# A pair's seventh operand formed earlier, its low parts on VectorE, and its last product behind the next pair's first, in the second layer's seven-product stages

## The chip, the cores and the metric

The kernel runs on one core of one Trainium2 chip. The time is that of one execution on the device, in microseconds (us). Three runs of the kernel before gave 2354.08, 2358.27 and 2360.64; the median, 2358.27, is its time.

## The reference, cut to what matters

Two layers (DEPTH = 2) of a mixer and a SwiGLU run over 512 latent tokens and 256 context tokens. The second layer needs only the latent tokens. The stages that the change touches are the branch gates' projection `g` and the two first projections of the SwiGLU, all of them products of the layer's activations with a large weight matrix:

```
def merge_branches(ys, g, w_branch, w_out):
    proj = jnp.einsum('bngi,gio->bngo', y, w_branch)
    gate = jax.nn.sigmoid(g.reshape(b, n, N_BRANCH, D_MODEL)...)
    return jnp.sum(gate * proj, axis=2) @ w_out

def swiglu(h, w_gate, w_up, w_down):
    return (jax.nn.silu(h @ w_gate) * (h @ w_up)) @ w_down
```

Here D_MODEL is 1024 and the SwiGLU's hidden width 2816, which is 22 blocks of 128 columns.

## The kernel before, in words

Every fp32 factor is split into a high part, rounded to TensorE's fp32r format, and a low part, the difference. A product of two factors is three matmuls: high by high, low by high, high by low. ScalarE casts a weight tile of 128x512 to its high part (`whi`, L220); a subtraction on VectorE or GpSimd makes the low part (`wlo`, L221).

For two neighbouring blocks of 128 output columns (a pair), the kernel doesn't multiply eight quarter matrices but seven, after Strassen and Winograd. The function `seven` (L478) lays out these products. The pair's weights are two tiles of 128x1024, `r0` and `r1`, of which each holds two quarters: a11 and a12, a21 and a22. `quarter` (L224) forms the weight operand of product q = 0 to 6: a11; a11 - a21 (written over a21); the sum s2 = a21 + a22 - a11; a12; the sum s1 = a21 + a22; a22; and a12 - s2, written over a12. L230 is the first sum s1, which needs both tiles; L231, L234 and L236 are the subtractions. The activations' sums (`tp`) are formed once for a stage by `sums` (L432 on). A product is 12 matmuls (four slices of 128 rows, three matmuls each), 84 for a pair. In layer 1 such a matmul has 384 columns (half of 768 tokens), in layer 2 256.

The products gather in three PSUM banks: the first, third, fifth and last in one (`y`), the second and sixth in another, the fourth in a third. ScalarE copies what a bank holds after the first three products (`p`, L491), and VectorE adds these copies back: L497 after the fourth product, L500 after the fifth, L502 after the sixth. So the last product's matmuls may not write bank `y` before the add at L500 has read it. In the FFN, gate pairs then go through the SiLU on ScalarE; the results of up pairs are multiplied by it, two of them on GpSimd (L1984) and one on VectorE (L1976).

`LO_POOL` tells which of a pair's seven low parts GpSimd forms: the first, fourth and sixth in layer 1, the fourth alone in layer 2. All others are VectorE's.

Weights come from HBM by loads of 512 KB on SyncE's queue (L213). They go round a ring of tiles, `raw` and `xraw`: four in layer 1, five in layer 2. A load waits until the tile that it overwrites has been read for the last time. `split_to` (L240) orders the loads and operands: a step asks for its own operand and the next four.

The stages are lists of steps, and a scheduler then sets each engine's order by a timeline of its own; within an engine, instructions run in that order. Some groups of steps are pinned against each other; the pairs' products are not.

In the FFN (L1892 on) the pairs run for f = 2, 4, ..., 20, each time gate then up: 20 pairs. After f = 12, layer 2 reloads two hidden tiles (`reload`). Ahead of the pairs lie two columns in the plain manner (L287, L296); behind them comes the down projection (L2056). The gate pairs of layer 2's mixer (L1606 on) are five.

Of the kernel before, what the change touches and what calls it, by code (L numbers as in the profile page):

```python
# [29 lines left out]
NF = FH // P  # L30
# [16 lines left out]
MID = ((), (3,))  # L47
PB = 1
PB = 1
LO_POOL = ((0, 3, 5), (3,))  # L50
MOD_NA = (4, 5)
MOD_FFN = ((8, 9), (10, 11))
THP = 2
# [90 lines left out]
class Kern:  # L144
# [37 lines left out]
    def drive(self):  # L182
        nc = self.nc
# [33 lines left out]
        def split(x, n, hi_eng, lo_eng, l=None):  # L217
            hi = ring(l, [P, 512], "whi", F32R, WB, XW)
            lo = ring(l, [P, 512], "wlo", F32R, WB, XW)
            hi_eng(hi[:, :n], x)  # L220
            lo_eng.tensor_sub(lo[:, :n], x, hi[:, :n].bitcast(F32))  # L221
            return hi, lo

        def quarter(pair, q):  # L224

            r0, r1 = raw[pair.r0], raw[pair.r0 + 1]
            a11, a12, a21, a22 = r0[:, :512], r0[:, 512:], r1[:, :512], r1[:, 512:]
            if q == 1:
                pair.sums[1] = self.t("fx", [P, 512], "ss", F32, 3)
                nc.vector.tensor_add(pair.sums[1], a21, a22)  # L230
                nc.vector.tensor_sub(a21, a11, a21)  # L231
            elif q == 2:
                pair.sums[2] = self.t("fx", [P, 512], "ss", F32, 3)
                nc.vector.tensor_sub(pair.sums[2], pair.sums[1], a11)  # L234
            elif q == 6:
                nc.vector.tensor_sub(a12, a12, pair.sums[2])  # L236
            x = (a11, a21, pair.sums.get(2), a12, pair.sums.get(1), a22, a12)[q]
            return Block([split(x, 512, nc.scalar.copy, nc.gpsimd if q in LO_POOL[pair.l] else nc.vector, pair.l)], 512)

        def split_to(n):  # L240
            while state[1] < min(n, len(reqs)):
                i = state[1]
                src, k, kind, r, pool, lo = reqs[i]
                if kind == "pair":
                    load_to(src.r0 + RAWB + XRAW[src.l])
                    got[i] = quarter(src, k)
                    if k == 6:
                        load_to(src.r0 + 1 + RAWB + XRAW[src.l])
                else:
                    load_to(r + 1)  # L250
                    x = raw.pop(r)
                    size = 416 if k == 832 else min(k, 512)
                    got[i] = Block([split(x[:, c:c + size], size, nc.gpsimd.tensor_copy if pool else nc.scalar.copy,
                                          nc.vector if lo else nc.gpsimd) for c in range(0, k, size)], size)
                    load_to(r + RAWB)
                state[1] += 1
# [221 lines left out]
    def seven(self, l, src, tp, dest, direct, added):  # L478
# [28 lines left out]
        def product(q, n, k, c):  # L507
# [16 lines left out]
        n_to_t = {6: 2, 7: 3, 4: 4}  # L524
        return [product(q, n, k, c) for q, (n, k, c) in enumerate(
            ((1, 0, e), (7, 0, None), (6, 0, None), (2, 4, e), (5, 0, d), (4, 0, None), (3, 4, d)))]


    def mod_steps(self, l, nb):
# [1362 lines left out]
    def ffn(self, l):  # L1892
# [70 lines left out]
        def pair_steps(up, f0):  # L1963
# [17 lines left out]
            def added(i, cols):  # L1981
                t = dest(i)[:, cols]
                if up:
                    nc.gpsimd.tensor_mul(t, t, s["sg", f0 + i][:, cols])  # L1984
                    if i == 1:
                        h_done(f0 + i)
                else:
                    nc.scalar.activation(t, t, AF.Silu)
# [23 lines left out]
                hs[f] = self.t("fd" if cx else "hk", [P, tt], f"h{f}")  # L2012
                nc.sync.dma_start(hs[f], self.hbuf[f][:, :tt])

        main = []
        for f in range(2, NF, 2):
            main += pair_steps(False, f) + pair_steps(True, f)
            if f == NA - 2 and not cx:
                main += [Step(reload)]
        st += main  # L2020
        st += [self.close("ft", "fx"), self.open("fd", "right")]

        if cx:
# [220 lines left out]
```

## Time and profile before

| what | value |
|---|---|
| median of three runs | 2358.27 us |
| the profiled execution's time | 2349.7 us |
| its span, first to last instruction | 2347.9 us |
| TensorE matmuls busy | 2258.5 us, 96% |
| VectorE busy | 1288.7 us, 55% |
| ScalarE busy | 1097.6 us, 47% |
| GpSimd busy | 922.7 us, 39% |
| mean granted TensorE clock | 0.989 |
| layer 2's gate pairs | 1783 to 1838 us of the span |
| layer 2's FFN pairs | 1985 to 2210 us of the span |

PE is TensorE, DVE VectorE, ACT ScalarE, POOL GpSimd, SP SyncE, which here only issues loads. In a group of instructions, `out<-in` are the program's names; after the bar come busy time, mean ns of one, and the idle time of the engine just before them with what ended it. A name such as `raw<-in_w_up_dram` is a load. Line numbers are those of the kernel before; in the order of the changed kernel they are 1 to 9 higher.

### The profile page before, as it was taken

The numbers are of one execution on the slowest core, as the hardware profiler recorded it, in microseconds if no ns is written. First come the engines' busy times: TensorE is split into PE (matmuls) and PEld (weight loads), VectorE is DVE, ScalarE is ACT, GpSimd is POOL, SyncE is SP. The second block draws the span as 40 slices with busy tenths as digits, with TensorE's granted clock in tenths as the row PEclk, the third lists the DMA queues.
The fourth block names the chain that finished last, engine by engine and source line by source line (L and its number), as shares of the span: only waits on it lengthen the run. The fifth ranks groups of instructions, "written<-read, shape, count | busy, mean of one in ns | idle before, by whom it ended". The sixth has DMA issues, their size and how long they took to land. (4 is left out here: it accounts for less than half of the span.)

```text
span 2347.9 us, 36358 instructions
## 1 busy us (share of the span) xinstructions
PE 2258.5 (96%) x13806; PEld 1960.9 (84%) x13806; DVE 1288.7 (55%) x2403; ACT 1097.6 (47%) x2434; POOL 922.7 (39%) x685
## 2 busy tenths in 40 slices
PE   7999999999999999999999999999999999999997
PEld 5877788878998889999987888787778878999875
DVE  7345456655424487556532272445578257888544
ACT  5346567634422254444442253675675325545532
POOL 1231153112258434334448362325301773323483
PEclk9999999999999999999999999999999999999998
DMA  9366321117676432222162342223224843323342
GB/s 356 117 228 217 126 95 62 68 63 268 210 275 227 142 135 84 99 99 86 63 246 72 108 155 83 76 89 100 79 73 176 299 153 139 117 93 103 111 153 63
DMA packets 113466, 323.43 MB, mean 138 GB/s; under 512 B 12966, under 2 KB 24172, under 8 KB 113292
## 3 DMA queue, kind: packets, MB, share of 16 engines
q1 hardware_dynamic: 89900, 269.34, 33.1%
q10 hardware_dynamic: 20160, 46.49, 5.2%
q0 software_dynamic: 3232, 5.28, 0.8%
q8 instruction: 108, 1.77, 0.3%
q14 instruction: 66, 0.54, 0.1%
HBM read 269.92 MB, written 55.35 MB: 139 GB/s over the span
## 5 line engine op out<-in xcount | busy, mean ns | idle before, releaser
L221 POOL TENSOR_TENSOR wlo<-raw,whi 128x512 fp32r<-128x512 f32 (+2 forms) x413 | 572.3, 1393 | 895.3 <-ACT whi L220 833.0
L220 ACT CAST whi<-raw 128x512 fp32r<-128x512 f32 (+1 forms) x449 | 274.0, 616 | 441.4 <-PE ps L1702 86.4
L519 PE MATMUL ps<-tp,whi 128*128 128x384 f32 (+1 forms) x1088 | 267.6, 315 | 0.2 <-ACT whi L220 0.2
L519 PE MATMUL ps<-AH,whi 128*128 128x384 f32 (+1 forms) x628 | 197.1, 316 | 7.2 <-DVE hx L500 4.1
L287 PE MATMUL ps<-AH,whi 128*128 128x512 f32 (+1 forms) x616 | 195.0, 362 | 3.3 <-ACT AH L738 3.3
L519 PE MATMUL ps<-AH,wlo 128*128 128x384 f32 (+1 forms) x628 | 196.4, 313 | 0.0
L519 PE MATMUL ps<-AL,whi 128*128 128x384 f32 (+1 forms) x628 | 194.8, 312 | 0.0
L519 PEld LDWEIGHTS ps<-tp,whi 128*128 128x128 f32 x1088 | 191.0, 189 | 2.1 <-PE ps L519 0.4
L287 PE MATMUL ps<-AH,wlo 128*128 128x512 f32 (+1 forms) x616 | 190.7, 357 | 0.0
L287 PE MATMUL ps<-AL,whi 128*128 128x512 f32 (+1 forms) x616 | 190.1, 356 | 0.0
L519 PE MATMUL ps<-tp,wlo 128*128 128x384 f32 (+1 forms) x544 | 171.0, 314 | 0.6 <-DVE wlo L221 0.6
L2056 PE MATMUL ps<-whi,hx 128*128 128x512 f32 x520 | 161.9, 390 | 7.3 <-DVE hx L2049 3.3
L335 PE MATMUL ps<-wlo,AH 128*128 128x512 f32 (+1 forms) x352 | 135.2, 384 | 0.8 <-POOL wlo L221 0.8
L335 PE MATMUL ps<-whi,AL 128*128 128x512 f32 (+1 forms) x352 | 135.7, 385 | 0.0
L335 PE MATMUL ps<-whi,AH 128*128 128x512 f32 (+1 forms) x352 | 134.0, 388 | 1.6 <-ACT whi L220 1.6
L519 PEld LDWEIGHTS ps<-AH,whi 128*128 128x128 f32 x628 | 119.0, 190 | 11.6 <-DVE hx L500 5.0
L287 PEld LDWEIGHTS ps<-AH,whi 128*128 128x128 f32 x616 | 105.4, 190 | 27.3 <-issue 7.7
L2056 PEld LDWEIGHTS ps<-whi,hx 128*128 128x128 f32 x520 | 97.5, 188 | 29.7 <-DVE hx L2049 3.7
L287 PEld LDWEIGHTS ps<-AL,whi 128*128 128x128 f32 x616 | 104.0, 189 | 19.6 <-issue 2.0
L519 PEld LDWEIGHTS ps<-AH,wlo 128*128 128x128 f32 x628 | 119.5, 190 | 0.1
L519 PEld LDWEIGHTS ps<-AL,whi 128*128 128x128 f32 x628 | 119.2, 190 | 0.0
L287 PEld LDWEIGHTS ps<-AH,wlo 128*128 128x128 f32 x616 | 104.4, 190 | 17.2 <-issue 1.5
(339 smaller groups left out, 5528.4 us busy)
## 6 DMA issues: line engine op xcount, KB each, us to landing
mraw<-in_w_mod_dram SPq DMA_DIRECT2D x80, 512.0 KB
raw<-in_w_down_dram SPq DMA_DIRECT2D x44, 512.0 KB
raw<-in_w_g_dram SPq DMA_DIRECT2D x42, 512.0 KB
raw<-in_w_up_dram SPq DMA_DIRECT2D x36, 512.0 KB
raw<-in_w_gate_dram SPq DMA_DIRECT2D x26, 512.0 KB
raw<-in_w_br_dram SPq DMA_DIRECT2D x24, 512.0 KB
gb<-th ACTq DMA_DIRECT2D x24, 384.0 KB
th<-gb SPq DMA_DIRECT2D x24, 384.0 KB
```

What stands on the lines that cost most here:

```text
L220: hi_eng(hi[:, :n], x)
L221: lo_eng.tensor_sub(lo[:, :n], x, hi[:, :n].bitcast(F32))
L287: self.nc.tensor.matmul(ps, w.at(wt, ws), at[:, k0 + kc, cols], start=kc == 0 and i == 0, stop=kc == nk - 1 and i == 2)
L335: self.nc.tensor.matmul(ps, a[:, k0 + kc, tok], w.at(b, ws), start=kc == 0 and i == 0, stop=kc == 2 * nb - 1 and i == 2)
L519: nc.tensor.matmul(ps, ws[0].at(wt, w), act[at], start=new and kc == 0 and i == 0, stop=kc == 3 and i == 2, skip_group_check=True)
L2056: nc.tensor.matmul(ps, h[a][:, tok], w.at(b, ws), start=f == seq[0] and i == 0, stop=f == NF - 1 and i == 2)
```

## The change

Three things are edited.

The seventh operand, a12 - s2, is written over s2 and no longer over a12, and it is formed right behind another operand of the pair: the sixth in layer 1, the fourth in layer 2 (`S4_AT`). The load that reuses tile `r0` is asked for there, too.

In layer 2 the fourth operand's low part goes from GpSimd to VectorE (`LO_POOL`), and so do the two multiplications of an up pair (L1984).

In layer 2's FFN, `crossed` puts a pair's last product behind the next pair's first, over the twelve pairs ahead of the reload and over the eight behind it.

```
-LO_POOL = ((0, 3, 5), (3,))
+LO_POOL = ((0, 3, 5), ())
+S4_AT = (5, 3)
...
-            elif q == 6:
-                nc.vector.tensor_sub(a12, a12, pair.sums[2])
-            x = (a11, a21, pair.sums.get(2), a12, pair.sums.get(1), a22, a12)[q]
-            return Block([split(x, 512, nc.scalar.copy, nc.gpsimd if q in LO_POOL[pair.l] else nc.vector, pair.l)], 512)
+            x = (a11, a21, pair.sums.get(2), a12, pair.sums.get(1), a22, pair.sums.get(2))[q]
+            b = Block([split(x, 512, nc.scalar.copy, nc.gpsimd if q in LO_POOL[pair.l] else nc.vector, pair.l)], 512)
+            if q == S4_AT[pair.l]:
+                nc.vector.tensor_sub(pair.sums[2], a12, pair.sums[2])
+            return b
...
-                    if k == 6:
+                    if k == S4_AT[src.l]:
                         load_to(src.r0 + 1 + RAWB + XRAW[src.l])
...
+    def crossed(self, pairs):
+
+        out = list(pairs[0])
+        for p in pairs[1:]:
+            out[-1:] = [p[0], out[-1]] + p[1:]
+        return out
...
-                    nc.gpsimd.tensor_mul(t, t, s["sg", f0 + i][:, cols])
+                    (nc.gpsimd if cx else nc.vector).tensor_mul(t, t, s["sg", f0 + i][:, cols])
...
-        main = []
-        for f in range(2, NF, 2):
-            main += pair_steps(False, f) + pair_steps(True, f)
-            if f == NA - 2 and not cx:
-                main += [Step(reload)]
-        st += main
+        if cx:
+            for f in range(2, NF, 2):
+                st += pair_steps(False, f) + pair_steps(True, f)
+        else:
+            prods = [pair_steps(up, f) for f in range(2, NF, 2) for up in (False, True)]
+            st += self.crossed(prods[:NA - 2]) + [Step(reload)] + self.crossed(prods[NA - 2:])
```

How this moves instructions, at three places. The first is VectorE late in layer 2's FFN pairs, before. `raw_4490` is a pair's first weight tile; the load of `raw_4562` goes into the same memory, and L230 reads it:

```order
L236 TENSOR_TENSOR raw_4490_22176<-raw_4490_22176,ss_4547_22493 128x512
L500 TENSOR_TENSOR h17_4141_20305<-ps_4530_22397,p7_4535_22429 128x256
L221 TENSOR_TENSOR xwlo_4561_22570<-raw_4490_22176,xwhi_4560_22569 128x512
L221 TENSOR_TENSOR wlo_4557_22550<-raw_4512_22297,whi_4556_22549 128x512
L221 TENSOR_TENSOR wlo_4571_22615<-xraw_4538_22436,whi_4570_22614 128x512
L221 TENSOR_TENSOR wlo_4575_22635<-ss_4573_22632,whi_4574_22634 128x512
L230 TENSOR_TENSOR ss_4594_22749<-raw_4562_22573 128x512
```

The same place in the changed kernel, where the tiles are `raw_4487` and `raw_4552`, and L231 is the first sum, L239 the seventh operand, L1993 the multiplications:

```order
L222 TENSOR_TENSOR wlo_4551_22514<-raw_4487_22158,whi_4550_22513 128x512
L499 TENSOR_TENSOR h16_4141_20307<-ps_4543_22458,p1_4530_22396 128x256
L222 TENSOR_TENSOR wlo_4556_22536<-ss_4544_22473,whi_4555_22535 128x512
L1993 TENSOR_TENSOR h16_4141_20307<-h16_4141_20307,hx_4518_22332 128x256
L502 TENSOR_TENSOR h17_4142_20308<-ps_4529_22383,p7_4536_22432 128x256
L235 TENSOR_TENSOR ss_4573_22632<-ss_4569_22611,xraw_4511_22295 128x512
L222 TENSOR_TENSOR wlo_4558_22553<-raw_4502_22242,whi_4557_22552 128x512
L504 TENSOR_TENSOR h17_4142_20308<-ps_4535_22419,p6_4540_22452 128x256
L222 TENSOR_TENSOR xwlo_4563_22574<-raw_4511_22295,xwhi_4562_22573 128x512
L1993 TENSOR_TENSOR h17_4142_20308<-h17_4142_20308,hx_4522_22354 128x512
L222 TENSOR_TENSOR xwlo_4566_22592<-ss_4547_22493,xwhi_4565_22591 128x512
L231 TENSOR_TENSOR ss_4594_22749<-raw_4552_22518 128x512
```

The last reader of the old tile stood three rows ahead of the sum that needs the new one; now it stands ten rows ahead.

The second place is GpSimd in the same stage, before: the fourth operands' low parts and the multiplications of up pairs.

```order
L1984 TENSOR_TENSOR h10_4133_20295<-h10_4133_20295,hx_4362_21492 128x256
L1984 TENSOR_TENSOR h11_4134_20296<-h11_4134_20296,hx_4366_21514 128x512
L221 TENSOR_TENSOR wlo_4421_21813<-raw_4358_21473,whi_4420_21812 128x512
L1984 TENSOR_TENSOR h12_4135_20297<-h12_4135_20297,hx_4412_21768 128x256
L221 TENSOR_TENSOR xwlo_4447_21954<-xraw_4384_21612,xwhi_4446_21953 128x512
L1984 TENSOR_TENSOR h13_4136_20298<-h13_4136_20298,hx_4416_21790 128x512
L1919 TENSOR_TENSOR hs131_4445_21950<-h13_4136_20298,hs130_4444_21949 128x512
```

In the changed kernel the stage's rows on GpSimd are these, between the stage ahead (`AL`) and the down projection's first low part:

```order
L405 TENSOR_TENSOR AL_70<-at_4080_19987,AH_69 128x4x128
L1928 TENSOR_TENSOR hs131_4445_21950<-h13_4137_20301,hs130_4444_21949 128x512
L1928 TENSOR_TENSOR hs121_4450_21974<-h12_4136_20300,hs120_4449_21973 128x512
L222 TENSOR_TENSOR wlo_4641_23005<-raw_4587_22710,whi_4640_23004 128x512
L222 TENSOR_TENSOR wlo_4643_23009<-raw_4587_22710,whi_4642_23008 128x512
```

Only two subtractions of hidden tiles are left there.

The third place is TensorE between two pairs of that stage, before; of each product its first matmul stands here, and of the fifth of the older pair (bank `ps_4348`, the first row) its last. `ps_4352` is that pair's sixth product; `ps_4374` and `ps_4378` are the next pair's first and second:

```order
L519 MATMUL ps_4348_21418<-AL_70,whi_4346_21414 128x256
L519 MATMUL ps_4352_21437<-tp41_4108_20217,whi_4350_21433 128x256
L519 MATMUL ps_4374_21557<-AH_69,xwhi_4359_21475 128x256
L519 MATMUL ps_4378_21576<-tp30_4105_20198,whi_4364_21498 128x256
L519 MATMUL ps_4348_21418<-AH_69,xwhi_4354_21453 128x256
```

The same pairs in the changed kernel, where the older pair's sixth product lies ahead of its fifth, and `ps_4387` is the next pair's fourth:

```order
L521 MATMUL ps_4347_21404<-AL_70,whi_4349_21419 128x256
L521 MATMUL ps_4373_21543<-AH_69,xwhi_4356_21457 128x256
L521 MATMUL ps_4379_21579<-tp30_4105_20198,whi_4364_21498 128x256
L521 MATMUL ps_4387_21618<-AH_69,whi_4370_21536 128x256
L521 MATMUL ps_4347_21404<-AH_69,xwhi_4359_21475 128x256
```

Between the fifth product's end and the last product's start stood 34 matmuls before and stand 31 here; over the 20 pairs of the stage the mean goes from 27 to 30. Outside of the four stretches of pairs (both layers' gate pairs and FFN pairs) the order of the two kernels is the same on every engine, but for a few rows at their edges. In layer 1's gate pairs one load of gate weights moves ahead of three loads of modulation weights (L583) on SP.

## The prediction

> **What bounds the kernel now.** I read the page's shares first, then the busy time by stage (which stretches have slack at all), then who TensorE waited for in those stretches, then what held the engine it waited for. The page:
>
> ```profile
> span 2347.9 us, 36358 instructions
> PE 2258.5 (96%) x13806; PEld 1960.9 (84%) x13806; DVE 1288.7 (55%) x2403; ACT 1097.6 (47%) x2434; POOL 922.7 (39%) x685
> ```
>
> TensorE works 96% of the span, so an edit beside the matmuls can only win back its idle time and the stretches in which its clock is halved. The change touches four stretches, which the matmuls of L519 mark out: layer 1's gate pairs (548 to 676 us), its FFN pairs (890 to 1190), layer 2's gate pairs (1783 to 1838) and layer 2's FFN pairs (1985 to 2210). Busy time by stretch; after each stretch's length come PE, PEld, DVE, ACT and POOL, the granted clock, the DMA share and GB/s:
>
> ```profile
> 548.00:676.00 128.00, 123.32 (x812) 112.13 (x811) 54.82 (x99) 50.74 (x94) 36.04 (x25) 0.99 0.63 225
> 890.00:1190.00 300.00, 300.00 (x1706) 298.83 (x1705) 167.90 (x234) 129.53 (x238) 127.30 (x87) 1.00 0.28 96
> 1783.00:1838.00 55.00, 51.44 (x422) 50.18 (x421) 40.33 (x72) 32.48 (x71) 13.44 (x10) 1.00 0.42 143
> 1985.00:2012.00 27.00, 25.50 (x166) 23.21 (x165) 25.80 (x55) 16.14 (x38) 10.49 (x4) 0.94 0.32 107
> 2012.00:2210.00 198.00, 192.10 (x1569) 189.30 (x1568) 153.93 (x242) 101.33 (x213) 60.86 (x45) 0.99 0.31 104
> 1999.60:2003.10 3.50, 3.50 (x19) 3.50 (x18) 3.50 (x8) 1.27 (x3) 0.72 (x1) 0.51 0.63 239
> 2132.70:2136.20 3.50, 3.50 (x17) 3.50 (x18) 2.08 (x4) 2.13 (x5) 0.00 (x0) 0.51 0.51 170
> ```
>
> Layer 1's FFN pairs have nothing to give (300.00 of 300.00). Layer 2's have, and twice inside them the clock is at 0.51 for 3.5 us, which costs 0.49 x 3.5 = 1.7 us each time. Who TensorE waited for, first in layer 2's FFN pairs (1985 to 2212), then in its gate pairs (total, times, longest):
>
> ```profile
> PE ps L519 <- DVE hx L500: 4.1, 3, 2.5
> PE ps L519 <- ACT whi L220: 1.5, 1, 1.5
> PE ps L519 <- DVE xwlo L221: 1.2, 1, 1.2
> PE ps L519 <- DVE h L500: 0.4, 2, 0.2
> PE ps L519 <- DVE th L500: 1.3, 2, 0.7
> PE ps L519 <- POOL xwlo L221: 1.1, 1, 1.1
> PE ps L519 <- DVE wlo L221: 0.6, 1, 0.6
> ```
>
> L500 is VectorE's add of the fifth product out of the PSUM bank into which the last product must go. So TensorE waits 7.2 us in the FFN pairs and 3.0 here in the gate pairs, almost all for VectorE. The longest of these waits, on VectorE and on TensorE:
>
> ```profile
> 2128.97 0.41 DVE L497 TENSOR_TENSOR hx<-ps,p 128x256 f32<-128x256 f32 x1
> 2129.30 1.71 DVE L236 TENSOR_TENSOR raw<-raw,ss 128x512 f32<-128x512 f32 x1
> 2130.94 0.68 DVE L221 TENSOR_TENSOR xwlo<-ss,xwhi 128x512 fp32r<-128x512 f32 x1
> 2131.54 0.68 DVE L234 TENSOR_TENSOR ss<-ss,raw 128x512 f32<-128x512 f32 x1
> 2132.14 0.41 DVE L500 TENSOR_TENSOR hx<-ps,p 128x256 f32<-128x256 f32 x1
> 2132.61 0.48 PE L519 MATMUL ps<-AH,whi 128*128 128x256 f32 x1 [2.48 <-DVE hx L500]
> ```
>
> The add takes 0.41 us; it is late because VectorE works in order and runs behind. (Starts 0.60 us apart are the price of an undisturbed 128x512 operation, 0.33 that of a 128x256 one.) What held VectorE in 1990 to 2210:
>
> ```profile
> DVE ss L230 <- DMA raw<-in_w_gate_dram: 8.6, 5, 2.5
> DVE ss L230 <- DMA xraw<-in_w_up_dram: 6.4, 3, 3.1
> DVE ss L230 <- DMA raw<-in_w_up_dram: 4.9, 4, 1.9
> DVE wlo L221 <- ACT whi L220: 4.7, 10, 0.9
> DVE ss L230 <- DMA xraw<-in_w_gate_dram: 2.0, 2, 1.8
> ```
>
> Fourteen times, 21.9 us in all, it stood at L230, a pair's first sum, for the pair's second weight tile. The other brake is GpSimd: operations of one shape take twice as long beside it. VectorE's first three rows here are of 2012 to 2210, then GpSimd's:
>
> ```profile
> L230 DVE TENSOR_TENSOR ss<-xraw 128x512 f32<-128x512 f32 x7 | 8.9, 1267 | 8.5 <-DMA xraw<-in_w_up_dram 6.4 <-DMA xraw<-in_w_gate_dram 2.0
> L231 DVE TENSOR_TENSOR xraw<-xraw,xraw 128x512 f32<-128x512 f32 x3 | 2.0, 682 | 0.0
> L502 DVE TENSOR_TENSOR h<-ps,p 128x256 f32<-128x256 f32 x10 | 4.1, 412 | 0.0
> L221 POOL TENSOR_TENSOR wlo<-raw,whi 128x512 fp32r<-128x512 f32 x15 | 21.2, 1416 | 38.8 <-ACT whi L220 37.1 <-DVE h L1976 1.5 <-PE ps L519 0.2
> L1984 POOL TENSOR_TENSOR h<-h,hx 128x512 f32<-128x512 f32 x10 | 15.1, 1514 | 29.3 <-DVE h L500 19.0 <-ACT p L491 6.5 <-DVE h L502 3.8
> ```
>
> **The change part by part.** TensorE's work stays: 84 matmuls a pair. What they cost when nothing waits, and how long a weight tile takes from issue to landing (the quickest and one of the slowest), the chain of waits tells:
>
> ```profile
> 2173.08 27.72 PE ps L519 x232
> 2027.37 3.40 DMA raw<-in_w_up_dram
> 2155.51 4.66 DMA xraw<-in_w_up_dram
> ```
>
> 27.72 / 232 = 0.1195 us, so a pair takes TensorE 10.0 us.
>
> *Seventh operand beside the fourth.* No instruction is added: the subtraction writes the sum's tile in place of the weights. It frees a pair's first weight tile at the fourth operand, not at the seventh, and the load behind it on SP's queue starts that much sooner. In the order shown above, 3 full-width operations (1.8 us) stood between the one that frees the tile and the L230 which needs its successor; now 10 rows do, 4 half-width and 6 full-width: 4 x 0.33 + 6 x 0.60 = 4.9 us. Against a landing of 3.4 to 4.7 us the stall goes from 1.6 to 2.9 us (21.9 / 14 = 1.6 is what the waits give) to about nothing. Counted so over all pairs, the middle distance goes from 1.5 to 4.6 us, with three or four pairs left at 3.1 or less: perhaps 3 to 5 us of the 21.9 remain. SP's queue holds only loads there, so an earlier place holds nothing else up.
>
> *Low parts and products on VectorE.* GpSimd loses 20 subtractions and 20 multiplications in the FFN pairs and 5 subtractions in the gate pairs; two subtractions of h remain in the FFN. VectorE gains 20 x 0.60 + 10 x 0.60 + 10 x 0.33 = 21.3 us there. Undisturbed, VectorE now has 10 full-width operations and 3 half-width ones a pair, 7.0 us, 7.3 with an up pair's product. The window's 153.93 us for 18.4 pairs (its 1569 matmuls less some 24 of the next stage, over 84) are 8.4 a pair, so the disturbance costs some 1.2. After it: 11 x 0.60 + 3 x 0.33 = 7.6 us for a gate pair, 11 x 0.60 + 5 x 0.33 + 0.60 = 8.9 for an up pair, 8.2 in the mean. VectorE is thus hardly lightened; it stays 1.1 us under TensorE's 10.0 even in an up pair. What covers the added work is this spare and the vanished stalls. The Trainium skill ("SBUF — State Buffer", section "SBUF: two separate sides") calls the port that VectorE and GpSimd share an exclusive lock: against a GpSimd operation one with two SBUF inputs blocks for the whole instruction. If each of the window's 45 GpSimd operations cost its full mean of 60.86 / 45 = 1.35 us, 61 us would come back, 3.3 a pair; the trace's 1.2 a pair says that most find VectorE elsewhere, and I go by the trace.
>
> *Last product behind the next pair's first.* By itself I cost this at nothing: the order before already had a mean of 27 matmuls (3.3 us) between a fifth product and its last, and now has 30. Bounds: 3 x 0.12 = 0.4 us more slack for each wait for L500, at most the 4.5 us of those waits, which I book under the first edit; a loss is excluded only as far as VectorE keeps up (rival below).
>
> *The start of the FFN pairs.* VectorE works without a pause from 1985 to 2012 (25.80 of 27), and TensorE waits 1.5 and then has the first halved clock, 1.7. Two low parts come onto that chain (1.2 us); what leaves is the wait for GpSimd and one stretched operation:
>
> ```profile
> 1989.46 0.69 DVE L236 TENSOR_TENSOR xraw<-xraw,ss 128x512 f32<-128x512 f32 x1 [1.20 <-POOL wlo L221]
> 1999.43 1.18 DVE L454 TENSOR_TENSOR tp<-t,tp 128x256 fp32r<-128x256 f32 x1
> ```
>
> 1.2 - 1.20 - (1.18 - 0.33) = -0.8. Ends: -3.2 (the whole wait and its halved clock) to +1.2. I take -0.8.
>
> *Gate pairs of layer 2.* They aren't crossed, so the 1.3 us for L500 stay. The 1.1 us for GpSimd go, and of the 0.6 for a low part half: -1.4. Ends: -3.0 to +1.2 (two more subtractions ahead of the first products).
>
> *Layer 1.* Operand formed at the sixth place, loads one place sooner, nothing waits in the FFN. In the gate pairs one weight load is now ahead of three loads of modulation weights on SP:
>
> ```profile
> PE ps L542 <- DMA mraw<-in_w_mod_dram: 3.8, 1, 3.8
> ```
>
> Those three come after the ones behind which TensorE stood, so 0; the end is one load's 512 KB at that stretch's 225 GB/s, +2.3.
>
> *The sum.* Of the 5.7 us of waits for VectorE in the pairs (4.1 + 1.2 + 0.4) I leave 1.0 for the stalls that remain: -4.7, ends 0 and -5.7. The halved clock at 2132.7 follows the 2.48 us wait at once and goes with it: -1.7, ends 0 and -1.7. With -0.8 and -1.4 that is -8.6; all good ends give -13.6, all bad ones +4.7. The Trainium skill ("TensorE: Matmul & The Clock Gate", section "What's actually happening") lets the clock fall only after an idle window of about 3.4 us; here it fell behind a wait of 2.48, and behind one of 1.5 with slow matmuls beside it, so the trace has a laxer condition. If the halved stretch came by that rule and not from this wait, the sum would be -6.9.
>
> The profiled execution took 2349.7 us, 8.6 below the median of 2358.27 (2354.08 to 2360.64). Against its own time the sum gives 2341.1; on the median's scale 2349.7, which is what I predict. 0.3% of it, about what a measurement of this kernel can tell from no change, is 7.1 us: faster begins at 2351.2, slower at 2365.3.
>
> **The rivals.**
>
> *Half of it.* VectorE's added work takes the place of the stalls. For it speaks that VectorE's sum hardly falls (8.4 to 8.2 a pair) and that its waits for ScalarE (4.7 us) stay; against it, that it was the late tile and not the mean load that made it fall behind. If half of the 4.7 and the halved clock stay, and the start gains nothing: -2.4 - 1.4 = -3.8, so 2354.5.
>
> *VectorE becomes the bound in the up pairs.* The multiplications now stand in VectorE's own order, 8.9 of 10.0 us; if waits of more than 1.1 us a pair stay, TensorE runs at VectorE's pace in ten pairs. Before, the waits for tiles and ScalarE were (21.9 + 4.7) / 20 = 1.3 a pair. At 2.5 a pair this costs 10 x (2.5 - 1.1) = 14 us against 5.7 of waits that it replaces: +8, so 2366. It decides from 1.7 a pair (10 x 0.6 = 6, no gain). Against it: the distances above, under which the tile's part of these waits goes.
>
> *A modulation load comes late.* If the load put ahead of three others on SP holds up the L542 matmuls, the 2.3 us come off the gain: -6.3, so 2352.
>
> *The crossing does nothing.* The distances of 27 and 30 matmuls say so, and my sum holds none of it; this alone moves no time.
>
> **How the numbers follow.** The forecast gets 0.53, half of it 0.32, the late load 0.08, VectorE as the bound 0.07. The first is faster, the second and third within 0.3%; of the fourth about 0.05 lies above 2365.3 and the rest within: faster 0.53, same 0.42, slower 0.05. The range reaches from the good end of the sum, 2358.3 - 13.6 = 2344.7, widened by 1.7 for a halved clock more or less, to where half a gain is lost to a bad start and a late load, 2354.5 + 1.2 + 2.3 = 2358, widened the same: 2343 to 2360.
>
> **What would show it.** In the profile after: the waits of VectorE's first sum for weight tiles in layer 2's FFN pairs under 6 us (21.9 now); GpSimd nearly empty there; VectorE's 128x512 operations at 0.68 us listed, none at 1.7; TensorE's waits for L500's successor under 2 us; no stretch at half clock after 2012. Wrong would be waits for VectorE that keep their sum with VectorE without a pause in the up pairs, or new waits in layer 1's gate pairs.

## The result, and the profile after

The changed kernel takes 2341.94 us (median of six runs, 2338.93 to 2346.97); the kernel before, run beside it, 2359.44 (median of six, one of which took 3168.29 us and isn't in the ratio). The ratio of the others is 0.9934, with a 95% interval of 0.9920 to 0.9948: 15.6 us off (12.3 to 18.9). The forecast was 8.6 off. The direction was right, the gain is nearly twice as large, and the time lies 1.1 us under the low end of the range.

In what follows, the change of a kernel's time in us is (ratio - 1) x 2358. The changed kernel's profiled execution took 2343.46 us. Its shares, from the page:

```profile
span 2341.7 us, 36357 instructions
PE 2262.3 (97%) x13806; PEld 1958.9 (84%) x13806; DVE 1306.4 (56%) x2448; ACT 1097.2 (47%) x2434; POOL 853.4 (36%) x640
```

GpSimd has 45 instructions and 69 us less, VectorE 45 and 18 us more, and ScalarE and TensorE have the same number as before. Now the busy time by stretch, in the prediction's columns: layer 1's gate and FFN pairs, layer 2's gate and FFN pairs, each from the first matmul of the pairs to the last. Behind them, in a fence of its own, layer 2's FFN pairs of the kernel before, cut in the same way:

```profile
548.60:671.50 122.90, 121.96 (x807) 110.43 (x806) 57.32 (x99) 49.94 (x93) 36.51 (x25) 1.00 0.64 233
888.50:1188.40 299.90, 299.69 (x1704) 298.54 (x1703) 168.64 (x230) 126.03 (x236) 133.21 (x88) 1.00 0.28 94
1784.80:1837.40 52.60, 51.39 (x422) 50.33 (x421) 40.45 (x77) 32.76 (x72) 7.57 (x6) 1.00 0.44 147
1989.00:2201.50 212.50, 211.44 (x1728) 208.28 (x1727) 181.74 (x335) 120.62 (x250) 12.01 (x9) 1.00 0.34 112
```

```profile
1985.70:2210.10 224.40, 217.00 (x1727) 211.93 (x1726) 179.04 (x295) 117.03 (x250) 71.34 (x48) 0.98 0.31 104
```

Layer 2's FFN pairs became 11.9 us shorter, and no halved clock is left in them. TensorE is busy for 211.44 of 212.50 us. VectorE works 2.7 us *more* than before in a stretch that is shorter by 11.9, so its mean load rose from 80% to 86%. Who TensorE waited for there (1980 to 2212), and then in layer 2's gate pairs (1770 to 1845):

```profile
PE ps L2065 <- ACT hx L2057: 1.2, 1, 1.2
PE ps L521 <- ACT whi L221: 1.0, 1, 1.0
...
PE ps L521 <- DVE th L502: 0.5, 1, 0.5
PE ps L521 <- ACT p L493: 0.5, 2, 0.2
PE ps L521 <- ACT whi L221: 0.2, 1, 0.2
```

(The row of L2065 is the down projection's.) No wait for VectorE or GpSimd is left in the FFN pairs: 1.0 us, for ScalarE, stands where 7.2 stood. And what VectorE waited for (1980 to 2205), the longest four:

```profile
DVE h L499 <- PE ps L521: 7.8, 6, 4.9
DVE wlo L222 <- ACT whi L221: 7.4, 15, 1.4
DVE h L1985 <- PE ps L521: 5.5, 2, 4.8
DVE xwlo L222 <- ACT xwhi L221: 4.2, 9, 1.1
```

The 21.9 us for weight tiles are gone, without one row left; VectorE now waits for ScalarE's casts and for TensorE's products, as an engine does that has caught up.

Some of the operations' durations, VectorE's groups and then GpSimd's (2005 to 2190):

```profile
L231 DVE TENSOR_TENSOR ss<-raw 128x512 f32<-128x512 f32 x10 | 6.9, 687 | 0.2
L231 DVE TENSOR_TENSOR ss<-xraw 128x512 f32<-128x512 f32 x8 | 6.5, 807 | 0.1
L1993 DVE TENSOR_TENSOR h<-h,hx 128x512 f32<-128x512 f32 x9 | 6.2, 684 | 0.1
...
L1928 POOL TENSOR_TENSOR hs<-h,hs 128x512 fp32r<-128x512 f32 x2 | 3.2, 1596 | 141.0 <-ACT hs L1927 141.0
L222 POOL TENSOR_TENSOR wlo<-raw,whi 128x512 fp32r<-128x512 f32 x1 | 1.3, 1290 | 63.2 <-ACT whi L221 63.2
```

The first sum L231 out of `xraw` took 1267 ns in the mean before and takes 807 now, with one long operation among its eight. That one, and the only other long one in the FFN pairs behind their first 25 us, stand in the timeline beside GpSimd's two last operations there, GpSimd's rows first, VectorE's behind them (start, duration):

```profile
2117.88 1.50 POOL L1928 TENSOR_TENSOR hs<-h,hs 128x512 fp32r<-128x512 f32 x1 [138.10 <-ACT hs L1927]
2122.26 1.69 POOL L1928 TENSOR_TENSOR hs<-h,hs 128x512 fp32r<-128x512 f32 x1 [2.88 <-ACT hs L1927]
...
2117.54 0.68 DVE L222 TENSOR_TENSOR wlo<-ss,whi 128x512 fp32r<-128x512 f32 x1
2118.26 1.67 DVE L231 TENSOR_TENSOR ss<-xraw 128x512 f32<-128x512 f32 x1
2119.85 0.68 DVE L222 TENSOR_TENSOR wlo<-raw,whi 128x512 fp32r<-128x512 f32 x1
...
2122.71 0.42 DVE L499 TENSOR_TENSOR hx<-ps,p 128x256 f32<-128x256 f32 x1
2123.04 1.46 DVE L222 TENSOR_TENSOR xwlo<-raw,xwhi 128x512 fp32r<-128x512 f32 x1
2124.42 0.68 DVE L222 TENSOR_TENSOR xwlo<-ss,xwhi 128x512 fp32r<-128x512 f32 x1
```

GpSimd's end at 2119.38 and 2123.95; VectorE's operations that began meanwhile end at 2119.93 and 2124.50, 0.55 us later in both cases, nearly an operation's undisturbed time. The add at L499, which has one operand in PSUM, runs at its usual 0.42 in the middle of GpSimd's second one. The Trainium skill ("SBUF — State Buffer", section "SBUF: two separate sides") calls the port that both share an exclusive lock, held for a whole instruction by whichever began first, and names VectorE's operations with two SBUF inputs: these rows agree with it.

I counted this over whole traces: VectorE's 128x512 operations in layer 2's FFN pairs (the same window as the groups'), with and without a GpSimd operation of over 0.5 us that overlaps them.

| kernel | beside GpSimd: count, mean, over 1 us | alone: count, mean, longest |
|---|---|---|
| before | 51, 1121 ns, 26 | 124, 683 ns, 695 ns |
| after | 4, 1126 ns, 2 | 208, 684 ns, 694 ns |

Alone, no operation was ever stretched. In the kernel before, all 26 long ones lay beside GpSimd; the 51 together cost 51 x (1121 - 683) = 22 us of VectorE's time. Whether TensorE waits for that time is another question, which the experiments answer.

### The profile page after: what moved, and what is told of

Same layout as the page of the kernel before. It is cut to its first block, busy times and chain, and to the rows that moved or that the text cites. A ratio compares the mean times of both kernels' runs of the same rounds, so it can differ in the third digit from the quotient of the medians.

```text
span 2341.7 us, 36357 instructions
## 1 busy us (share of the span) xinstructions
PE 2262.3 (97%) x13806; PEld 1958.9 (84%) x13806; DVE 1306.4 (56%) x2448; ACT 1097.2 (47%) x2434; POOL 853.4 (36%) x640
## 5 line engine op out<-in xcount | busy, mean ns | idle before, releaser
L222 POOL TENSOR_TENSOR wlo<-raw,whi 128x512 fp32r<-128x512 f32 (+2 forms) x400 | 551.6, 1386 | 968.9 <-ACT whi L221 917.6
L221 ACT CAST whi<-raw 128x512 fp32r<-128x512 f32 (+1 forms) x435 | 265.0, 616 | 420.9 <-PE ps L1711 84.0
L521 PE MATMUL ps<-tp,whi 128*128 128x384 f32 (+1 forms) x1088 | 263.6, 314 | 1.2 <-ACT whi L221 1.0
L521 PE MATMUL ps<-AH,whi 128*128 128x384 f32 (+1 forms) x628 | 195.1, 313 | 0.5 <-ACT whi L221 0.2
L521 PE MATMUL ps<-AH,wlo 128*128 128x384 f32 (+1 forms) x628 | 194.9, 311 | 0.2 <-POOL wlo L222 0.2
L521 PE MATMUL ps<-AL,whi 128*128 128x384 f32 (+1 forms) x628 | 194.0, 310 | 0.0
L521 PEld LDWEIGHTS ps<-tp,whi 128*128 128x128 f32 x1088 | 189.1, 188 | 3.0 <-ACT whi L221 1.2
L2065 PE MATMUL ps<-whi,hx 128*128 128x512 f32 x520 | 165.2, 398 | 7.5 <-DVE hx L2058 3.4
L521 PE MATMUL ps<-tp,wlo 128*128 128x384 f32 (+1 forms) x544 | 170.3, 314 | 0.0
L2065 PEld LDWEIGHTS ps<-whi,hx 128*128 128x128 f32 x520 | 99.7, 192 | 30.5 <-DVE hx L2058 3.8
L521 PEld LDWEIGHTS ps<-AH,whi 128*128 128x128 f32 x628 | 117.9, 188 | 3.5 <-issue 1.2
L521 PEld LDWEIGHTS ps<-AH,wlo 128*128 128x128 f32 x628 | 118.1, 188 | 0.8 <-POOL wlo L222 0.5
L521 PEld LDWEIGHTS ps<-AL,whi 128*128 128x128 f32 x628 | 117.9, 188 | 0.0
```

The lines of the kernel that those rows point to most:

```text
L521: nc.tensor.matmul(ps, ws[0].at(wt, w), act[at], start=new and kc == 0 and i == 0, stop=kc == 3 and i == 2, skip_group_check=True)
L2065: nc.tensor.matmul(ps, h[a][:, tok], w.at(b, ws), start=f == seq[0] and i == 0, stop=f == NF - 1 and i == 2)
```

## The experiments

Three theories stood against each other. A: the late weight tile made VectorE late, and the first edit (seventh operand beside the fourth) brings the gain; this was the prediction's. B: the crossing brings it. C: GpSimd's operations slow VectorE's, and the second edit (low parts and multiplications to VectorE) brings it; C2, a form of it: what counts is that GpSimd's own slow results are waited for. The kernels are variants of the two known ones, so line numbers differ by a few: the matmuls of the pairs are L519 before and L521, L525 or L529 in the others.

| kernel | ratio to before, interval | us | layer 2's gate + FFN pairs in its profile, us |
|---|---|---|---|
| before (two profiles) | 1 | 0 | 55.1 + 224.4, 54.5 + 224.3 |
| after (two profiles) | 0.9934 [0.9920, 0.9948] | -15.6 | 52.6 + 212.5, 53.3 + 212.5 |
| first edit alone | 0.9978 [0.9963, 0.9993] | -5.2 | 59.1 + 220.1 |
| first edit, layer 1 alone | 0.9985 [0.9972, 0.9998] | -3.5 | 55.0 + 224.5 |
| second edit alone | 0.9932 [0.9919, 0.9944] | -16.0 | 56.2 + 210.2 |
| its multiplications alone | 0.9979 [0.9964, 0.9994] | -5.0 | 55.2 + 220.9 |
| its low parts alone | 0.9965 [0.9949, 0.9980] | -8.3 | 56.9 + 218.8 |
| crossing alone | 0.9985 [0.9971, 0.9998] | -3.5 | 55.1 + 223.7 |
| all but the second edit | 0.9977 [0.9965, 0.9989] | -5.4 | 58.8 + 217.6 |
| all but the crossing | 0.9938 [0.9921, 0.9956] | -14.6 | 52.6 + 213.1 |
| second edit, GpSimd repeats the old work | 1.0000 [0.9985, 1.0016] | 0.0 | 55.2 + 226.4 |
| second edit, GpSimd does free work | 0.9980 [0.9965, 0.9994] | -4.7 | 57.8 + 215.0 |

### The first edit alone

The kernel before with the first edit, in both layers (cut):

```
+S4_AT = (5, 3)
...
+            if q == S4_AT[pair.l]:
+                nc.vector.tensor_sub(pair.sums[2], a12, pair.sums[2])
...
-                    if k == 6:
+                    if k == S4_AT[src.l]:
```

> The first edit alone, in both layers: the seventh operand is formed early over the sum's tile, and the load behind it starts sooner; GpSimd keeps its low parts and multiplications, the last products are not crossed. Theory A (VectorE was late because it stood at a pair's first sum for a late weight tile): most of the gain comes with this, 8 to 11 us off the 2359.4 of before, and VectorE's waits for tiles at that sum in layer 2's FFN fall from 21.9 us to under 6. Theory B (the crossing gives TensorE the slack): 0 to 3 us off. Theory C (GpSimd's operations slow VectorE, and that made it late): the waits for tiles fall, but TensorE still waits about 5 us in the FFN pairs, 2 to 5 us off.

It gained 5.2 us. The late tiles did go: VectorE's waits at its first sum, in 1985 to 2212, and then TensorE's waits there and in layer 2's gate pairs (1783 to 1843):

```profile
DVE ss L231 <- DMA raw<-in_w_up_dram: 2.8, 3, 1.7
...
DVE ss L231 <- DMA xraw<-in_w_up_dram: 1.5, 4, 0.6
DVE ss L231 <- DMA raw<-in_w_gate_dram: 1.3, 4, 0.4
...
DVE ss L231 <- DMA xraw<-in_w_gate_dram: 0.6, 2, 0.4
...
PE ps L521 <- POOL wlo L222: 4.9, 1, 4.9
PE ps L521 <- DVE xwlo L222: 0.6, 1, 0.6
...
PE ps L521 <- POOL xwlo L222: 2.9, 1, 2.9
PE ps L521 <- DVE th L502: 2.8, 1, 2.8
```

21.9 us of waits for tiles became 6.2, a little over the 3 to 5 of the prediction. TensorE still waits 6.5 us in the FFN pairs (7.2 before), and the gate pairs got 4 us longer, which takes back the 4.3 that the FFN pairs won: 59.1 + 220.1 is 279.2, and the kernel before has 279.5 and 278.8. What this run gained can then be layer 1's alone, and theory A, which puts most of the gain here, fails by the total.

Where the 6.5 us lie says more. All of them stand in the first 24 us of the FFN pairs. Behind that, where the tiles had been late, TensorE doesn't stand once; its row there (columns as above), and then the longest wait at the start, on GpSimd and on TensorE:

```profile
2020.00:2212.00 192.00, 192.00 (x1597) 191.00 (x1596) 157.27 (x244) 107.61 (x219) 64.31 (x46) 1.00 0.33 106
```

```profile
2007.71 8.66 POOL L222 TENSOR_TENSOR wlo<-raw,whi 128x512 fp32r<-128x512 f32 x1 [10.29 <-ACT whi L221]
...
2016.42 0.39 PE L521 MATMUL ps<-AH,wlo 128*128 128x256 f32 x1 [4.90 <-POOL wlo L222]
```

From the 253rd matmul of the pairs (three pairs' worth) to their end, the long part of the stage below, it takes 175.2 us, against 184.4 and 184.5 in the two profiles of before and 175.0 in those of the whole change. So there the first edit alone brings all that the whole change brings, with GpSimd busy for 64.31 us and 29 operations of VectorE over 1 us: theory A is right for this part. Up to that matmul it takes 44.9 us, against 40.0 and 39.8 before. What costs there is a low part of GpSimd that took 8.66 us while VectorE worked for all of them, and TensorE waited for it, as theory C2 says. The gate pairs show the same: of their 5.7 us of waits for VectorE and GpSimd 2.9 are for a low part of GpSimd, which took 4.65 us. Why this edit makes these low parts longer than before (2.58 us in the FFN, 1.73 in the gate pairs) isn't shown.

### The second edit alone

```
-LO_POOL = ((0, 3, 5), (3,))
+LO_POOL = ((0, 3, 5), ())
-                    nc.gpsimd.tensor_mul(t, t, s["sg", f0 + i][:, cols])
+                    (nc.gpsimd if cx else nc.vector).tensor_mul(t, t, s["sg", f0 + i][:, cols])
```

> The second edit alone: in layer 2 the fourth low part and the up pairs' multiplications go to VectorE; seventh operand and order of products as before. Theory A: the waits of VectorE for tiles at the first sum stay at 15 to 25 us and with them most of TensorE's waits, and VectorE has more to do: 0 to 4 us off. Theory C: VectorE loses its stretched operations and TensorE's waits in the FFN pairs fall under 3 us: 8 to 12 us off. Theory B: nothing, or slower by the 8.9 us of work in an up pair.

It gained 16.0 us, as much as all three edits, and more than theory C's 8 to 12. The FFN pairs without their start, by engine, and then TensorE's waits in 1988 to 2205 and VectorE's for tiles:

```profile
2016.00:2201.00 185.00, 185.00 (x1549) 184.28 (x1548) 153.79 (x280) 103.79 (x214) 10.78 (x8) 1.00 0.34 108
```

```profile
PE ps L525 <- ACT whi L222: 1.2, 2, 1.0
PE ps L525 <- DVE tp L460: 0.4, 1, 0.4
...
DVE ss L232 <- DMA xraw<-in_w_gate_dram: 3.4, 2, 2.6
DVE ss L232 <- DMA xraw<-in_w_up_dram: 3.4, 2, 1.9
DVE ss L232 <- DMA raw<-in_w_up_dram: 3.4, 4, 1.4
DVE ss L232 <- DMA raw<-in_w_gate_dram: 2.3, 3, 1.2
```

VectorE still stands 12.5 us for late tiles, and TensorE works 185.00 of 185.00 us. So the late tile alone doesn't make TensorE wait either: a VectorE that GpSimd doesn't hold up makes up for it. From the 253rd matmul of the pairs on, this kernel takes 172.3 us (1.3 of the gain are 11 matmuls of the down projection that the scheduler put behind the pairs here), and up to it 38.0. Either edit thus takes away the waits in the long part of the stage. Ahead of it the second edit alone wins 2 us where the first one alone loses 5; in the gate pairs it loses 1 or 2 us (56.2 against 55.1 and 54.5), the first one 4.

### The crossing alone, and layer 1 alone

```
+            st += self.crossed(prods[:NA - 2]) + [Step(reload)] + self.crossed(prods[NA - 2:])
```

> The third edit alone: in layer 2's FFN a pair's last product is emitted behind the next pair's first; operands and engines as before. Theory A: the scheduler had put some 27 matmuls between a fifth and a last product already, so 0 to 2 us off, TensorE's waits for VectorE in the FFN pairs stay at 5 to 8 us. Theory B: these waits fall under 2 us, 6 to 10 us off.

The crossing alone measured -3.5 us with an interval that nearly touches zero, and its layer 2 is the old one within 0.8 us (55.1 + 223.7). TensorE's waits for VectorE in its FFN pairs are 6.8 us. Without it the whole change gave -14.6 us, with it -15.6, with intervals that overlap almost entirely. Theory B falls. Where this run's 3.5 us come from isn't shown; they say how far a total of this size can be trusted.

Layer 1 alone is the kernel before with the first edit where `pair.l` is 0:

> Only layer 1's part of the first edit: its seventh operand is formed at the sixth place over the sum's tile, its loads start one operand sooner; layer 2 as before. If layer 1 gives nothing, as predicted (its FFN pairs had no wait): within 2 us of before. Rival: the load of modulation weights for which TensorE waited 3.8 us in layer 1's gate pairs comes in time and the halved clock after it goes: 4 to 6 us off, and the gate pairs take 123 us of the span and not 127.

It measured -3.5 us, between the 2 expected and the rival's 4 to 6, and its layer 2 is the old one (55.0 + 224.5). In its profile layer 1's gate pairs take 124.8 us, against 127.2 and 123.2 in the two profiles of before. These pairs vary: over the eight profiles with the old order in layer 1 they take 122.8 to 128.7, mean 125.5, and over the six with the new one 122.8 to 125.9, mean 124.1. What differs is the wait for modulation weights, which was 3.8 us in the profile of before: 0.8 to 3.8 with the old order (mean 2.3), 0 to 1.9 with the new (mean 0.9). So the profiles speak for 1 or 2 us, a difference that lies within the spread of either group. Why the modulation weights come sooner, with a weight load put ahead of three of them, wasn't found.

### GpSimd repeats its old work

The second edit alone; behind each low part and multiplication that went to VectorE, GpSimd forms the same thing again into a scratch tile that nothing reads:

```
+            if dup:
+                scr = self.t("fx", [P, 512], "scr")
+                nc.gpsimd.tensor_sub(scr[:, :n], x, hi[:, :n].bitcast(F32))
...
+                        nc.gpsimd.tensor_mul(scr[:, cols], t, s["sg", f0 + i][:, cols])
```

> The second edit alone, with GpSimd's old work done a second time: in layer 2 VectorE forms the fourth low part and the up pairs' products, and GpSimd repeats each of them behind it into a scratch tile that nobody reads. GpSimd is as busy as before, and nobody needs its results. Theory C (GpSimd's operations stretch VectorE's): most of the gain of the second edit alone (15.5 us) is lost, 2351 to 2360, with VectorE's full-width operations at 1.2 to 1.8 us again and TensorE waiting 4 us or more for VectorE in the FFN pairs. Theory C2 (it was GpSimd's own slow results, 1.4 to 1.5 us each, that somebody waited for): the gain stays, 2341 to 2346.

The whole gain is gone: ratio 1.0000. No result of GpSimd's repeats is used, so C2 can't account for this loss. The two waits on which TensorE lost most (1980 to 2212) and one of VectorE's:

```profile
PE ps L529 <- ACT whi L222: 4.2, 4, 1.6
PE ps L529 <- ACT xwhi L222: 2.1, 2, 1.6
...
DVE raw L242 <- POOL scr L226: 1.7, 2, 0.9
```

18 of VectorE's operations take over 1 us again, but theory C's other sign didn't come: TensorE waits 1.3 us for VectorE (4 or more were expected) and 6.6 for ScalarE. The last row may show why. The repeats read weight tiles, and L242, which overwrites such a tile, waits for them; ScalarE's casts stand behind L242. Also, the scheduler gave TensorE, VectorE and ScalarE another order than with the second edit alone. So the repeats might cost by holding tiles, or by the order, and not by stretching.

### GpSimd does work that holds no weight tile

The second edit alone; behind each SiLU and each multiplication of an up pair, GpSimd multiplies the result tile by itself into a scratch tile: 40 operations that read only hidden tiles and that nobody waits for. The order on all other engines is that of the second edit alone.

```
+                if not cx:
+                    scr = self.t("fx", [P, 512], "scr")
+                    nc.gpsimd.tensor_mul(scr[:, cols], t, t)
```

> The second edit alone, with 40 operations on GpSimd in layer 2's FFN pairs that nobody waits for: behind each SiLU and each up pair's multiplication GpSimd multiplies the result tile by itself into a scratch tile that nothing reads. Unlike the repeats of its old low parts they hold no weight tile, so no weight tile's reuse waits for GpSimd. Theory C in its strict form (the operations themselves stretch VectorE's): VectorE's 128x512 operations over 1 us come back, and most of the 15 us is lost, ratio 0.997 to 1.0. Rival (what costs is that GpSimd holds the tiles that it reads, so that VectorE's overwriting of a weight tile and ScalarE's next cast wait for it): the gain stays, 0.993 to 0.995.

The ratio is 0.9980, as theory C expected (0.997 to 1.0): 11.3 of the 16.0 us are gone again (6.8 to 15.8, from the two intervals). The row of the FFN pairs without their start, TensorE's waits in all of them, and a piece of the timeline, GpSimd's row and then VectorE's beside it:

```profile
2015.00:2210.00 195.00, 192.68 (x1606) 191.32 (x1605) 172.67 (x293) 104.91 (x221) 55.01 (x46) 1.00 0.33 103
```

```profile
PE ps L525 <- ACT p L497: 1.2, 1, 1.2
PE ps L525 <- ACT whi L222: 1.2, 2, 1.0
PE ps L525 <- DVE hx L506: 1.1, 2, 0.8
PE ps L525 <- DVE tp L460: 0.4, 1, 0.4
```

```profile
2066.52 0.93 POOL L2002 TENSOR_TENSOR scr<-h 128x256 f32<-128x256 f32 x1 [5.61 <-DVE h L1997]
...
2066.89 1.11 DVE L223 TENSOR_TENSOR wlo<-raw,whi 128x512 fp32r<-128x512 f32 x1
2067.92 0.41 DVE L506 TENSOR_TENSOR h<-ps,p 128x256 f32<-128x256 f32 x1
```

Of VectorE's 128x512 operations, counted as above, 23 are over 1 us again, all of them beside GpSimd (with the second edit alone: two); the 136 that ran alone took 683 ns. The one in the timeline ends 0.55 us behind GpSimd's end, as the two further above did. Two waits for the add at L506, L500's successor, are back. So operations of GpSimd on which no other engine depends do cost time: theory C in its strict form is shown. How much of the gain it accounts for is less sure.

The total says some two thirds, but the profile shows only 215.0 - 210.2 = 4.8 us of the 11.3 in the FFN pairs, a third of what the second edit won there, and 1.7 of these are a halved clock at the start. The rest of that execution's time against the second edit's lies in stretches whose code is the same (layer 2's gate pairs 1.6, layer 1's 3.4, the others 2.0), which differ from one execution to the next. What is left between this run and the repeats (0.9980 against 1.0000, intervals that overlap) may be the tiles held, the order, or that other operations meet.

### Half of the second edit

The 20 multiplications alone on VectorE, and the 25 low parts alone:

> Half of the second edit: in layer 2's FFN the up pairs' 20 multiplications go to VectorE, the fourth low parts stay on GpSimd. Theory C puts the gain in proportion to GpSimd's time that goes, some 24 of 60 us: 5 to 8 us off 2358.5. Theory C2: the multiplications' results are needed only at the stage's end, so nothing, within 2 us.

> The kernel before with only the subtractions of the second edit: layer 2's 25 fourth low parts on VectorE, the 20 multiplications of up pairs stay on GpSimd. Theory C (each GpSimd operation stretches VectorE's beside it, and the loss grows faster than in proportion once VectorE is behind): 20 of 45 operations of the FFN pairs stay, so part of the 15 us comes: ratio 0.994 to 0.997. If what counts were the results of the subtractions that TensorE waits for (C2), nearly the whole gain, 0.993. If the two parts simply add up (0.9932 for both, 0.9979 for the multiplications), 0.9953.

They gave -5.0 and -8.3 us. The sum, -13.3, is the whole edit's -16.0 within the intervals (3 us each), so with the old order of tiles the price can be the same for each GpSimd operation taken away: 16.0 / 45 = 0.36 us (0.25 for a multiplication, 0.33 for a low part). No sharp threshold shows at which VectorE falls behind.

### The whole change without one part

> The whole change without the second edit: operands early, last products crossed, but GpSimd keeps the fourth low parts and the multiplications in layer 2. If the first and third edits help together what neither does alone (3 us each at most): 6 to 9 us off 2358.5. Theory C: no more than the two apart, 3 to 6 us off, and TensorE still waits 4 us or more in the FFN pairs.

> The whole change without the crossing. Theory C and the count of the order (27 matmuls between fifth and last product before, 30 after) say the crossing is worth nothing: 2341 to 2345, as the whole change. If the crossing is what makes VectorE's later adds harmless once it has more to do: 2347 or more, with waits for L502's successor in the up pairs.

Without the second edit -5.4 us stay, as theory C expected (3 to 6); but of the 4.7 us that TensorE waits in the FFN pairs 4.3 are for GpSimd's low parts at the start and none for VectorE. Without the crossing it is -14.6. Beside the first edit, the second one is thus worth some 10 us. The first edit still has a use beside the second, in layer 2's gate pairs: 59.1 us with the first alone, 56.2 with the second alone, 52.6 and 53.3 with both. In the FFN pairs it adds nothing to the second (213.1 with both, 210.2 with the second alone, which has 11 matmuls of the down projection less among its pairs).

### Before and after once more

> The kernel before once more, for a second profile: total time at half clock and where it lies. If the halved stretches are set by the program, they lie at the same places and sum to 53 us again; if only those within layer 2's FFN pairs are (theory C: a wait of over a microsecond for a disturbed VectorE), these return and the others move or change in length by several us.

> The changed kernel once more, for a second profile: no half clock in layer 2's FFN pairs by theory C, GpSimd's busy time there 12 to 13 us, and a sum of halved stretches elsewhere that differs from the 58.6 us of the first profile by several us if they vary from execution to execution.

The second profiles took 2354.45 and 2336.13 us. Layer 2's FFN pairs reproduce: 224.4 and 224.3 before, 212.5 twice after. The rest, the same code in all four but for a few rows, doesn't: span less the four stretches of pairs is 1641.3 and 1650.7 before, 1653.9 and 1644.8 after. Between the two of after it is the clock: in total it is halved for 58.6 and 39.8 us, and half of the difference is 9.4. Between the two of before it is not: 53.4 and 52.1 us, of which 43.2 and 48.7 lie outside of the four stretches, account for 2.8 of the 9.4; waits for GpSimd's low parts ahead of the FFN, 0.8 and 3.1, for another 2.3. About the same 140 us ahead of layer 2's FFN in the two profiles of after (by engine, then granted clock):

```profile
1840.00:1980.00 140.00, 132.38 (x641) 103.60 (x639) 72.62 (x103) 45.76 (x83) 89.23 (x68) 0.96 0.59 209
```

```profile
1836.00:1976.00 140.00, 133.89 (x669) 106.81 (x669) 72.06 (x107) 46.37 (x84) 93.15 (x69) 0.99 0.62 216
```

One has a halved stretch of 10.24 us there, the other one of 3.41. Of the two halved stretches in layer 2's FFN pairs before, the second profile has the one behind the wait of 2.5 us and not the one at the start, and the pairs take as long.

## Why the prediction was right and wrong

*Size of the terms.* Layer 2's FFN pairs were to win 4.7 + 1.7 + 0.8 = 7.2 us and won 11.9 (11.8 between the second profiles). The first two terms belong to the long part of the stage, which won 9.4 and not 6.4; the third to its start, which won 2.5 (2.3 between the second profiles) and not 0.8. Over all of the pairs TensorE's waits give 7.2 - 1.0 = 6.2 and the halved clock about 3 (in the second profiles it is 7.5 and half of 3, with one halved stretch less). The remaining 2.3 to 3 are matmuls that started late without a recorded wait or halved clock: 78 started over 0.06 us late before, 56 after. The sum had no term for these. Layer 2's gate pairs were to win 1.4 and won 2.5 and 1.2. Layer 1 was put at 0, with an end of +2.3; its own run gives 3.5, the profiles 1 to 2, not clear of chance. 11.9 + 1.9 + 1.4 is 15.2 against the measured 15.6.

*The step that failed* is "Low parts and products on VectorE". It saw the stretched operations, priced them rightly at 1.2 us a pair (22 us over some 18 pairs, as counted), and then set the 21.3 us of added work against them: "VectorE is thus hardly lightened". So it gave this edit nothing to win in the long part of the stage, and some 2 us in all at the start and in the gate pairs. As a mean that is right: VectorE's busy time in the FFN pairs even grew, from 179.04 to 181.74 us. But the edit alone won 16.0 us, and beside the first edit some 10. That an added operation costs less than a stretch of the same length, because it stands at a known place in VectorE's order and a stretch comes when GpSimd happens to be active, is a likely reason, and not measured.

*The late tile.* "It was the late tile and not the mean load that made it fall behind" is half right. In the long part of the stage the first edit alone does what the sum booked under it, and more: 9.2 us, and no wait of TensorE is left. But the second edit alone does the same there, with the tiles late. VectorE fell behind because two things held it up, and taking away either is enough. The step that the sum didn't see is that the first edit without the second one loses at the start and in the gate pairs what it wins behind them (4.9 and 4.0 us), where TensorE waits for low parts that GpSimd forms slowly. The prediction's row of that kind, 1.20 us at the start, was the small form of it.

*The exclusive lock.* The prediction weighed this rule of the Trainium skill ("SBUF — State Buffer", section "SBUF: two separate sides") as a total, 3.3 us a pair, against the trace's 1.2, and went by the trace. The count of 1.2 was right, and it doesn't speak against the rule, since only 51 of 175 operations met GpSimd. What both sums left out is that an operation that does can be late by 1.1 us at once (1.79 against 0.68), and that GpSimd's operations are held up, too (8.66 us for one low part).

*Scale.* The profiled execution of before was a quick one (2349.7, with a median of 2358.27); putting the sum on the median's scale was right, and the 7 us of gain that the sum lacked don't come from there.

*The rivals.* "Half of it" and "VectorE becomes the bound in up pairs" rested on VectorE's mean load and didn't come, although that load rose. "A modulation load comes late" has the opposite sign, as far as it shows: the wait was shorter in the mean. "The crossing does nothing" held.

*What would show it.* These are signs of the whole change, and they don't tell its edits apart. No wait for tiles (under 6 was asked), GpSimd at 4.48 us of 185 by its groups' sum (3.2 + 1.3), no wait for VectorE in the FFN pairs, and no half clock in them: all right. "128x512 operations at 0.68, none at 1.7" held but for two, of 1.67 and 1.46 us, and these two stand beside GpSimd's last operations.

## What to carry to other kernels

When VectorE feeds TensorE, work that GpSimd takes off it can cost more than it saves: here 45 GpSimd operations, all of whose work VectorE could do at no loss, cost some 16 us, and some 10 where the tiles came in time. Look in the groups for one shape with two durations, and put the long ones beside GpSimd's rows in the timeline; price such a hit where it lands and not as a mean. When two things hold an engine up, each edit alone can take all of the wait away, and the gains of single edits don't add up (5.2 and 16.0 against 15.6). And when a wait's total hardly changes (7.2 and 6.5 us), look where in the stage it lies before calling the theory wrong: here the old waits were gone, and others had come at the start.

## What the runs showed of the hardware

- A VectorE operation of 128x512 that has both operands in SBUF took 0.695 us at most when it ran alone (820 operations in the traces of before, after, the second edit alone and the two with work put back on GpSimd) and up to 1.79 beside a GpSimd operation. Of the 128x256 adds out of PSUM in the same traces 51 overlapped a GpSimd operation, and the longest took 0.427; alone it was 0.426. So the adds, which have one operand in PSUM, aren't stretched.
- It goes the other way as well. A GpSimd subtraction of 128x512 took 8.66 us (first edit alone, 2007.71 us) while VectorE was busy for all of them; behind the start of that stage 15 of the same kind took 1.37 us in the mean.
- Halved clock comes in stretches of 3.41 us and multiples (6.83, 10.24, 13.65), but for the last one of each profile, which runs past the last instruction. They lie at about the same places of the program in each execution but not always, and not equally long: 39.8 to 58.6 us in two executions of one kernel. The Trainium skill ("TensorE: Matmul & The Clock Gate", section "What's actually happening") tells of a window of 3413 ns that runs freely; the lengths agree with it. Behind the same wait of 1.50 us the clock fell in one profile of before and not in the other. A single profile's span can't tell a gain of under some 10 us here; the stretches of the pairs, compared one by one, can.
